# Hybrid decoder layer, fp32-accurate MLP: output tiles, token-tile turns, second-weight sums, norm rows and last chunks rearranged

## The chip, the cores and the metric

The kernel runs on one core of a Trainium2 chip. The metric is the device time of one execution in microseconds (us), as a median of several runs; lower is better. The core has five engines that run their own instruction queues: TensorE (PE, matrix products; its weight loads are listed as PEld), VectorE (DVE), ScalarE (ACT), GpSimd (POOL) and SyncE (SP, which here only issues DMAs). ACT and POOL issue DMAs too, each on its own queue. On chip there are the SBUF (128 partitions) and the PSUM, whose banks of 128x512 fp32 take the matrix products.

## The reference, cut to what matters

One layer for 1024 tokens of width 1024. A mixer (sliding-window attention beside a gated delta net) comes first; the change begins at its output projection and reaches to the end:

```python
mixed = (sigmoid(g_a) * y_a + sigmoid(g_b) * y_b) @ w_out[l]
x = _layer_norm(ALPHA * x + (1.0 + gt1) * mixed, ln1_g[l], ln1_b[l])
u2 = x * (1.0 + sc2) + sh2
h = jnp.square(jax.nn.relu(u2 @ w_ff1[l] + b_ff1[l]))          # 1024 -> 4096
x = _layer_norm(ALPHA * x + (1.0 + gt2) * (h @ w_ff2[l] + b_ff2[l]), ln2_g[l], ln2_b[l])
```

Everything is fp32 in and out.

## The kernel before

**Products.** An fp32 product is made of three faster ones: each operand is split into a high part (a rounded copy, made by ACT) and a low part (the remainder, made by DVE); PE adds high x high, high x low and low x high into one bank. The helper split_s (L213 and on) does it: ACT copies at once (L215), and DVE subtracts "lag" matmuls later (L216). Names such as wh and wl (weights), mh, ml, u11h and u11l (tokens) are such parts, and sp in the second layer.

**Seven products instead of eight.** Both MLP layers split their matrices in two by two blocks and use seven block products, whose operands are sums and differences of blocks. So DVE also forms sums of token tiles (T1 to T4), of the first weights (f_sums, f_sums2), of the hidden activations (h_sums, h_sums2, stored to the DRAM array hf_d), and of the second weights (t_make, stored to the DRAM array wt_d). The sums and differences are add_ (L1516) and sub (L1407).

**The order by hand.** Everything that DVE and ACT do beside the products is put into their queues by an events list: at(p, f) runs f when the count of matmuls has reached p, and after(n, f) runs it n matmuls later. So the order on PE, DVE and ACT is what the numbers say; an engine that waits holds up all that stands behind it in its queue. The order on the DMA queues of SP and POOL is settled by the framework when the kernel is built. E0 is the count at the start of the output projection of the mixer, F0 = E0 + 384 that at the start of the first MLP layer, and G0 = F0 + 1344 that of the second.

**Projection (E0 to F0).** Four segments of 96 matmuls give the eight token tiles of 128 tokens. mix_done (L1356 and on) adds the residual and takes the sums for the norm; ACT takes the root, DVE norms the tile, and then the tile is transposed ("turned") by PE (u2_turn, L1379) four 128x128 blocks at a time into a bank "b"; ACT puts each turned block from there into SBUF (L1382, "rawu<-b"), with the scale and the shift of the MLP. quad_split and t_split split the result, and the sums T1 to T4 are formed between (t_one, t_sums). Tiles 0 to 3 are turned in pairs of a first-half and a second-half tile, in blocks of 128x256 on ACT; tiles 4, 5, 6 and 7 one by one, in blocks of 128x128.

**First layer (F0 to G0).** 16 pairs of weight tiles ("pairs" 0 to 15), seven products each, 12 matmuls of 128x512 a product (L1841). The first five pairs (EARLY) run in an order of their own in which the products that need only early token tiles stand first. Each product ends in a bank with the name mm, a, b or c. ACT copies it with the bias into a "t" tile (part, L1558), or DVE adds it to one (full, L1516); ACT squares it (L1566, L1567; a last block L1577, L1578) and stores it to hf_d (L1554). The pool has six "t" tiles of 128x512, used in turn; one comes free when its store has landed and its other readers are done. t_load brings the second weights of pair n into two "wx" tiles and half an "sb" tile (on POOL's queue), t_make forms three differences "wx<-wx" and one "sb<-sb,wx" from them and stores them on the same queue.

**Second layer (G0 to the end).** 56 chunks of 24 matmuls (L1901). Each chunk loads an activation tile from hf_d and a weight tile ("sraw"): chunks 0 and 1 through ACT's queue, the others through SP's; s_split splits both. rows_load brings six rows of 128x1024 (gates and norm parameters, broadcast to all partitions); rows_sums combines three of them. The last seventh of the chunks goes chunk by chunk over four token tiles up to the last LAST = 4 chunks, which go tile by tile, so that a tile's gate, residual, norm and store (gated, norm2) can run while PE is on the next one. The last tile is cut in two halves of 256.

## Time and profile before

| | |
|---|---|
| median of 3 runs (lowest to highest) | 1829.93 us (1829.84 to 1831.34) |
| the profiled execution | 1830.36 us, span 1828.5 us, mean granted clock 0.994 |
| up to the first MLP layer | 0 to 1195.86 us |
| first layer, pairs 0 to 4 and the start of pair 5 | 1195.86 to 1300.75 us |
| first layer, the rest | 1300.75 to 1510.59 us |
| second layer | 1510.59 to 1818.49 us |
| after the last matmul | 1818.49 to 1828.5 us |

The span runs from the first to the last instruction of the profiled execution; 1.86 us lie around it. PE is busy nearly all the time, so the profile is read for the short moments in which PE waits. Rows of the timeline give start, duration, engine, line, operation, "out<-in" by the program's names, the shapes, and in brackets the idle time ahead of it with what ended it. Rows of the waits give the total, the number and the longest. Rows of the windows give, for a stretch, its length and each engine's busy time and instructions (PE, PEld, DVE, ACT, POOL), the granted clock, the DMA engines' share and the rate in GB/s.

### The profile page before, as it was taken

What the parts mean: (1) busy time and instruction counts of PE and PEld (TensorE: products, weight loads), DVE (VectorE), ACT (ScalarE), POOL (GpSimd) and SP (SyncE); (2) the same over time, 40 slices, a digit from 0 to 9 for tenths busy, and PEclk for the clock granted to TensorE, in tenths of its full rate; (3) what the DMA queues carried; (4) which work ended last, traced back from release to release, by engine and by line L of the source; (5) the groups of instructions that cost most, each with busy time, mean ns of one, the idle gap of its engine ahead of it and who ended that gap; (6) DMA issues with size and microseconds to landing.
All of it is one profiled execution on the core that took longest, in us unless ns stands there. A gap on an engine that the chain in (4) does not pass through costs nothing.

```text
span 1828.5 us, 26178 instructions
## 1 busy us (share of the span) xinstructions
PE 1806.0 (99%) x9161; PEld 1513.3 (83%) x9161; DVE 1262.5 (69%) x2377; ACT 1023.9 (56%) x2325; POOL 307.9 (17%) x464
## 2 busy tenths in 40 slices
PE   8999999999999999999999999999999999999997
PEld 6988888888888888888888888877888887888886
DVE  6688688888854666666644445887777766676697
ACT  4699678888864555555544222485555554434341
POOL 0233234453340000000001100012221120000000
PEclk8999999999999999999999999999999999999999
DMA  9756723232266555554447434369887779655571
GB/s 277 205 199 207 225 67 98 63 111 70 73 218 152 157 158 152 146 165 141 147 146 252 155 127 161 115 202 332 290 277 263 258 271 390 242 185 185 206 254 47
DMA packets 262670, 337.74 MB, mean 185 GB/s; under 512 B 26261, under 2 KB 171366, under 8 KB 262282
## 3 DMA queue, kind: packets, MB, share of 16 engines
q1 hardware_dynamic: 223210, 212.94, 37.1%
q0 software_dynamic: 31184, 106.34, 17.4%
q10 hardware_dynamic: 8144, 16.78, 2.6%
q8 instruction: 72, 1.18, 0.3%
q14 instruction: 60, 0.49, 0.1%
HBM read 231.40 MB, written 102.51 MB: 183 GB/s over the span
## 4 chain that ended last, share of the span: by engine, by line
PE 88%; DVE 3%; ACT 3%; DMA 2%; issue 0%; POOL 0%; ACTq 0%; DVEq 0%; POOLq 0%
PE mm L248 40%; PE mm L1841 7%; PE mm L1901 6%; PE b L1841 4%; PE b L1901 4%; PE a L1901 4%; PE a L1841 2%; PE mm L1470 2%; PE c L1901 2%; PE c L880 2%; PE a L1470 1%; DMA hf_d<-t 1%; PE mm L186 1%; PE mm L187 1%; PE mm L188 1%; PE a L806 1%
## 5 line engine op out<-in xcount | busy, mean ns | idle before, releaser
L248 PE MATMUL mm<-uh,wl 128*128 128x512 f32 x800 | 330.1, 413 | 0.0
L248 PE MATMUL mm<-ul,wh 128*128 128x512 f32 x800 | 314.7, 393 | 0.0
L248 PE MATMUL mm<-uh,wh 128*128 128x512 f32 x800 | 313.9, 392 | 0.0
L216 DVE TENSOR_TENSOR sp<-sraw,sp 128x1024 fp32r<-128x1024 f32 x112 | 132.8, 1220 | 77.9 <-ACT sp L215 77.8
L215 ACT ACTIVATE sp<-sraw 128x1024 fp32r<-128x1024 f32 x112 | 112.7, 1054 | 123.5 <-PE b L1901 75.3
L248 PEld LDWEIGHTS mm<-ul,wh 128*128 128x128 f32 x800 | 150.2, 188 | 31.8
L248 PEld LDWEIGHTS mm<-uh,wl 128*128 128x128 f32 x800 | 150.8, 188 | 26.3 <-issue 1.0
L248 PEld LDWEIGHTS mm<-uh,wh 128*128 128x128 f32 x800 | 150.9, 189 | 25.3 <-issue 1.0
L1901 PE MATMUL mm<-sp 128*128 128x512 f32 x528 | 137.0, 390 | 1.4 <-DVE sp L216 1.3
L1901 PEld LDWEIGHTS mm<-sp 128*128 128x128 f32 x528 | 98.5, 188 | 22.6 <-DVE sp L216 2.0
L216 DVE TENSOR_TENSOR wl<-wr,wh 128x1024 fp32r<-128x1024 f32 x81 | 99.4, 1228 | 8.5 <-ACT wh L215 8.4
L215 ACT ACTIVATE wh<-wr 128x1024 fp32r<-128x1024 f32 x81 | 85.2, 1052 | 22.1 <-PE c L1470 13.8
L1901 PE MATMUL a<-sp 128*128 128x512 f32 x336 | 92.6, 389 | 0.0
L813 DVE CUSTOM_DVE_ANT_0 nscore<-a,amask,nsink 128x256 f32<-128x256 f32 (+1 forms) x128 | 54.5, 464 | 44.8 <-PE a L806 44.5
L1901 PE MATMUL b<-sp 128*128 128x512 f32 (+1 forms) x336 | 80.0, 374 | 0.0
L1901 PEld LDWEIGHTS a<-sp 128*128 128x128 f32 x336 | 63.1, 188 | 13.1
L1142 ACT ACTIVATE vn<-a,brk 128x128 f32<-128x128 f32 x64 | 23.5, 368 | 89.0 <-PE a L1140 89.0
L1901 PEld LDWEIGHTS b<-sp 128*128 128x128 f32 x336 | 60.5, 188 | 11.2
L216 DVE TENSOR_TENSOR wl<-fraw,wh 128x1024 fp32r<-128x1024 f32 x43 | 52.6, 1223 | 23.2 <-ACT wh L215 22.9
L824 POOL TENSOR_TENSOR sm<-sm 128x256 f32<-128x256 f32 x56 | 50.8, 906 | 105.2 <-ACT sm L820 76.9
L215 ACT ACTIVATE wh<-fraw 128x1024 fp32r<-128x1024 f32 x43 | 45.0, 1056 | 33.1 <-PE b L1841 16.3
L820 ACT ACTIVATE sm<-nscore,stat 128x257 f32<-128x257 f32 (+1 forms) x128 | 62.0, 488 | 2.7 <-DVE stat L813 2.5
(522 smaller groups left out, 4662.0 us busy)
## 6 DMA issues: line engine op xcount, KB each, us to landing
wr<-in_w_in_dram SPq DMA_DIRECT2D x60, 512.0 KB, 3.8
sraw<-hf_d SPq DMA_DIRECT2D x54, 512.0 KB, 4.5
adaw<-in_w_ada_dram SPq DMA_DIRECT2D x73, 256.0 KB, 4.7
fraw<-in_w_ff_dram SPq DMA_DIRECT2D x32, 512.0 KB, 5.2
sraw<-wt_d SPq DMA_DIRECT2D x32, 512.0 KB, 4.3
hf_d<-t ACTq DMA_DIRECT2D x48, 256.0 KB, 3.5
wt_d<-wx POOLq DMA_DIRECT2D x48, 256.0 KB, 3.0
sraw<-in_w_ff_dram SPq DMA_DIRECT2D x22, 512.0 KB, 5.6
```

Of the source, the lines that this page charges most:

```text
L186: T.matmul(t, lhsT=wh[:, k, :], rhs=xh[k][:, sl], start=k == 0, stop=False)
L215: A.activation(out=hi, in_=src, func=AF.Copy)
L216: after(lag, lambda: V.tensor_tensor(out=lo, in0=src, in1=hi.bitcast(F32), op=ALU.subtract))
L248: T.matmul(ts[half], lhsT=w[:, k, :], rhs=xx[k][:, sl], start=k == 0 and m == 0, stop=k == KT - 1 and m == 2)
L813: V.tensor_tensor_reduce(out=ns[:, i, 1:1 + W], in0=sc[:, i * 2 * P:i * 2 * P + W], in1=amask[:, mo:mo + W], scale=-1.0, scalar=nsink[:, 2 ...
L820: A.activation(out=sm[:, i, 0:1 + W], in_=ns[:, i, 0:1 + W], func=AF.Exp, scale=-1.0, bias=st[:, i:i + 1], accum_out=st[:, 2 + i:3 + i])
L824: G.tensor_tensor(out=sm[:, :, 1 + P:1 + 2 * P], in0=sm[:, :, 1:1 + P], in1=sm[:, :, 1 + P:1 + 2 * P], op=ALU.add)
L880: T.matmul(av[:, 0:256], lhsT=vt[:, b, :], rhs=p_[:, m, :], start=p_ is full and m == 0, stop=p_ is prods[-1][1] and m == 1)
L1142: after(1, lambda: A.activation(out=vn, in_=Wp[:, 0:P], func=AF.Copy, scale=brk[:, n, h:h + 1]))
L1470: T.matmul(pt, lhsT=m[k][:, tok], rhs=w[:, k % 2, :], start=k == 0 and w is wh and m is mh, stop=k == KT - 1 and m is ml)
L1841: T.matmul(pt, lhsT=a[:, k0 + k, :], rhs=b[k], start=begin and k == 0 and x_ == 0, stop=k == 3 and x_ == 2, skip_group_check=True)
L1901: T.matmul(to, lhsT=a[:, f, t * P:(t + 1) * P], rhs=b[:, f, lo:up], start=(begin or own) and s % NS == 0 and f == 0 and x_ == 0, stop=s % ...
```

## The change

It has eight parts, in the words of the program:

1. Eight "t" tiles instead of six. To make room, the small tiles tri, trim, amask and the eleven tiles made by small() move from a pool that lives to the end into gp (through brief), a pool that is closed soon after the projection begins.
2. Tiles 4 and 5, and tiles 6 and 7, are turned together: pair_turn makes four turns of two blocks of each tile, and each turn is put by two ACT copies of 128x256 (16 copies of 128x128 a pair before). pair_quad and pair_split split pieces of the pair, in the order T1, block 22, sums, T2, T3, T4. The times of the events (29 and 44 after the last tile's end, the lags of mix_done and of the root) follow.
3. The first tile of the first weights is split 37 matmuls sooner, into four "t" tiles (W0).
4. t_make of the 16 pairs stands at the places of a table (MAKE), t_load 40 matmuls ahead of each.
5. The six norm rows go through SP's queue, one every 24 matmuls from G0 + 62; rows_sums moves from G0 + 60 to G0 + 190.
6. LAST = 5: five last chunks tile by tile.
7. The last chunk's two splits stand 6 matmuls apart instead of 10.
8. The norms of the first three tiles of the last product run over the whole width in one piece.

```diff
@@ -51,6 +51,11 @@
     big = ctx.enter_context(tc.tile_pool(name="big", bufs=1))
     ps = ctx.enter_context(tc.tile_pool(name="ps", bufs=2, space=PSUM))
     dram = ctx.enter_context(tc.tile_pool(name="dram", bufs=1, space=DRAM))
+    gp_pool = tc.tile_pool(name="gp", bufs=2, side="right")
+    gpool = gp_pool.__enter__()
+
+    def brief(shape, name):
+        return gpool.tile(shape, F32, name=name, bufs=1)
 
     def psum(tag, bufs, name=None):
...
-    tri = const.tile([P, P], F32, name="tri")
+    tri = brief([P, P], "tri")
...
@@ -1309,8 +1312,8 @@
     for f in range(KT):
         stream_unit(oh, ol, yb_done(f))
 
-    def row(dst, src):
-        nc.gpsimd.dma_start(out=dst, in_=src[None, :].partition_broadcast(P))
+    def row(dst, src, q=None):
+        (q or nc.gpsimd).dma_start(out=dst, in_=src[None, :].partition_broadcast(P))
 
     E0 = count[0]
...
         rq = r[:, halves[q]]
-        tm = pe.tile([P, HALF], F32, tag="t", name="tm", bufs=6)
+        tm = pe.tile([P, HALF], F32, tag="t", name="tm", bufs=8)
...
         V.bn_aggr(out=st[:, 0:2], in_=parts[:, t].rearrange("p q s -> p (q s)"))
-        lag = {6: 26, 7: 12}.get(t, 1)
+        lag = {6: 26, 7: 8}.get(t, 1)
...
@@ -1419,26 +1422,70 @@
             for k in range(4):
                 at(p + 12 + 3 * (4 * kh + k), t_split, j, kh, k)
 
+    rawp = {}
+
+    def pair_turn(u, ks):
+        if ks[0] == 0:
+            for kh in range(2):
+                rawp[kh, u] = big2.tile([P, 4, 2, P], F32, tag=f"{'hl'[kh]}{6 + u}", name="rawp")
+        tp = psum("b", 2)
+        for i, k in enumerate(ks):
+            for v in range(2):
+                T.transpose(tp[:, (2 * i + v) * P:(2 * i + v + 1) * P], rs[TILE[u][2 + v]][:, k * P:(k + 1) * P], ident)
+
+        def put(i, k):
+            A.activation(out=rawp[k // 4, u][:, k % 4].rearrange("p j c -> p (j c)"),
+                         in_=tp[:, 2 * i * P:2 * (i + 1) * P],
+                         func=AF.Identity, scale=sc2[:, k:k + 1], bias=sh2[:, k:k + 1])
+        for i, k in enumerate(ks):
+            after(2 + i, put, i, k)
+
+    def pair_quad(name, kh, u):
+        for i in range(2):
+            src = rawp[kh, u][:, 2 * i:2 * i + 2].rearrange("p k j c -> p k (j c)")
+            hi, lo = (t[i][:, :, 2 * P:4 * P] for t in U[name, "t"])
+            split_s(hi, lo, src, 4)
+
+    def pair_one():
+        sub(V, rawp[0, 1], rawp[0, 1], rawp[0, 0])
+
+    def pair_sums():
+        sub(V, rawp[1, 1], rawp[1, 1], rawp[0, 1])
+        sub(V, rawp[0, 0], rawp[1, 1], rawp[0, 0])
+        sub(V, rawp[1, 0], rawp[1, 0], rawp[1, 1])
+
+    def pair_split(kh, u, k):
+        hi, lo = (t[4 * kh + k].rearrange("p (j u c) -> p j u c", j=4, u=2)[:, 2:4, u, :] for t in (mh, ml))
+        split_s(hi, lo, rawp[kh, u][:, k], 3)
+
+    def pair_done(u, p):
+        for kp in range(4):
+            at(p + (4, 8)[u] * kp, pair_turn, u, (2 * kp, 2 * kp + 1))
+        if u == 0:
+            at(p + 8, pair_quad, "11", 0, 0)
+            at(p + 17, pair_quad, "21", 1, 0)
+            return
+        at(p + 14, pair_one)
+        for k in range(4):
+            at(p + 20 + 3 * k, pair_split, 0, 1, k)
+        at(p + 32, pair_quad, "22", 1, 1)
+        at(p + 39, pair_sums)
+        for n, (kh, v) in enumerate(((1, 1), (0, 0), (1, 0))):
+            for k in range(4):
+                at(p + (42, 66, 80)[n] + 3 * k, pair_split, kh, v, k)
+
     def u2_done(t, p):
 
         u = t in TILE[1]
         j = TILE[u].index(t)
-        if j < 2:
-            if not u:
-                return
+        if j == 3:
+            pair_done(u, p)
+        elif j < 2 and u:
             for kp in range(4):
                 at(p + 5 * kp, u2_turn, j, (0, 1), (2 * kp, 2 * kp + 1))
             at(p + 13, quad_split, j, "11", 0, 0)
             at(p + 23, quad_split, j, "21", 1, 0)
             u2_rest(j, p + 24)
-            return
-        for kp in range(2):
-            at(p + 6 * kp, u2_turn, j, (u,), range(4 * kp, 4 * kp + 4))
-        if u:
-            u2_rest(j, p + 14)
-        else:
-            at(p + 8, quad_split, j, "11", 0, 0)
-            at(p + 14, quad_split, j, "21", 1, 0)
 
     at(E0 + 15, open_pe)
...
@@ -1456,9 +1503,17 @@
         split_s(hl[0], hl[1], r[0])
 
 
+    W0 = []
+
+    def w_first():
+        raw = raws.pop(0)[0]
+        for kh in range(2):
+            W0.append([pe.tile([P, 4, P], F32R, tag="t", name="w0", bufs=8) for _ in "hl"])
+            split_s(W0[kh][0], W0[kh][1], raw[:, 4 * kh:4 * kh + 4, :], 5)
+
     w_more()
-    for p in [1, 13] + [SEG * s + o for s in (0, 2) for o in (61, 73, 86, 98)] + [3 * SEG + o for o in (79, 100, 118, 134, 154)]:
-        at(E0 + p, w_go)
+    for p in [1, 13] + [SEG * s + o for s in (0, 2) for o in (61, 73, 86, 98)] + [3 * SEG + o for o in (42, 98, 118, 134, 154)]:
+        at(E0 + p, w_first if p == 3 * SEG + 42 else w_go)
         at(E0 + p + 8, w_more)
 
...
@@ -1490,10 +1545,10 @@
                 for pt, t in zip(pts, ts):
                     mix_mm(pt, slice(t * P, (t + 1) * P), c)
             for pt, t in zip(pts, ts):
-                lag = 14 if s == 2 and t > 5 else 10 if s == 3 and t == 7 else 1
+                lag = {(2, 6): 14, (2, 7): 56, (3, 7): 10}.get((s, t), 1)
                 at(max(count[0] + lag, E0 + 28), mix_done, s % 2 == 1, q, t, pt)
                 if s % 2 == 1:
-                    at(count[0] + 1, u2_done, t, count[0] + {4: 30, 5: 36, 6: 48, 7: 42}.get(t, 34) - lag + 1)
+                    at(count[0] + 1, u2_done, t, count[0] + {5: 29, 7: 44}.get(t, 34) - lag + 1)
 
 
...
@@ -1673,10 +1728,10 @@
         for j, t in enumerate((t1, t2, t3, t4)):
             nc.gpsimd.dma_start(out=wt_d[j, n], in_=t)
 
+    MAKE = (172, 246, 320, 394, 484, 552, 620, 693, 767, 842, 916, 990, 1068, 1139, 1214, 1288)
     for n in range(NPAIR):
-        p = pos[n, 1] - 8 if n > EARLY else F0 + 100 + 68 * n
-        at(p, t_load, n)
-        at(p + 36, t_make, n)
+        at(F0 + MAKE[n] - 40, t_load, n)
+        at(F0 + MAKE[n], t_make, n)
 
 
...
@@ -1724,11 +1779,12 @@
             acc[t] = p2f.tile([P, D], F32, name=f"acc{t}", bufs=1)
         stats["all"] = p2f.tile([P, NT, 22], F32, name="stats", bufs=1)
 
-    def rows_load():
-        for n, (name, src) in enumerate((("gt2", gt_d[1]), ("G2", ln1_g), ("B2", b_ff2), ("lb", ln1_b), ("g2", ln2_g),
-                                         ("b2", ln2_b))):
-            rows_[name] = wp.tile([P, D], F32, tag="wl" if n % 2 else "wh", name=name)
-            row(rows_[name], src)
+    ROWS = (("gt2", gt_d[1]), ("G2", ln1_g), ("B2", b_ff2), ("lb", ln1_b), ("g2", ln2_g), ("b2", ln2_b))
+
+    def rows_load(n):
+        name, src = ROWS[n]
+        rows_[name] = wp.tile([P, D], F32, tag="wl" if n % 2 else "wh", name=name)
+        row(rows_[name], src, nc.sync)
 
     def rows_sums():
...
@@ -1796,7 +1852,7 @@
         after(3, rest)
 
     p15 = pos[NPAIR - 1, 1]
-    LAST = 4
+    LAST = 5
     for s in range(7 * NS):
         p = G0 + 24 * s
         at((p15 + 16, p15 + 28, p15 + 62, p15 + 64)[s] if s < 4 else p - 96 - 28, s_load, s)
@@ -1804,13 +1860,14 @@
             if s < 2:
                 q = p15 + (52, 68)[s] + 8 * j
             elif s >= 6 * NS:
-                q = p - (94 if s > 6 * NS else 70) + 10 * j
+                q = p - (94 if s > 6 * NS else 70) + (6 if s == 7 * NS - 1 else 10) * j
             else:
                 q = p - 46 + 10 * j
             at(q, s_split, s, j)
     at(G0 + 2, open_p2f)
-    at(G0 + 3, rows_load)
-    at(G0 + 60, rows_sums)
+    for n in range(6):
+        at(G0 + 62 + 24 * n, rows_load, n)
+    at(G0 + 190, rows_sums)
     for t in range(NT):
         at(G0 + 200 + 60 * t, rr_load, t)
...
@@ -1836,9 +1893,10 @@
         for k in range(4):
             for x_ in range(3):
                 run_events(count[0])
-                (wh, wl), (uh_, ul_) = WF[i, w], U[mv]
+                (wh, wl), (uh_, ul_) = W0[k0 // 4] if (i, w) == (0, "a") else WF[i, w], U[mv]
+                kk = k if (i, w) == (0, "a") else k0 + k
                 a, b = ((wh, uh_), (wh, ul_), (wl, uh_))[x_]
-                T.matmul(pt, lhsT=a[:, k0 + k, :], rhs=b[k], start=begin and k == 0 and x_ == 0,
+                T.matmul(pt, lhsT=a[:, kk, :], rhs=b[k], start=begin and k == 0 and x_ == 0,
                          stop=k == 3 and x_ == 2, skip_group_check=True)
                 count[0] += 1
...
@@ -1931,7 +1989,7 @@
                         for f in range(2):
                             step(s, f, t, lo, up)
                     after(1, gated, 4 + t, lo, up, 1 + i, (tail[0] if i else bank[t])[:, lo:up])
-                after(1, norm2, 4 + t, [(HALF, D), (0, HALF)], 1 + len(cuts) - 1)
+                after(1, norm2, 4 + t, [(0, D)] if t < 3 else [(HALF, D), (0, HALF)], 1 + len(cuts) - 1)
             break
         for _ in steps(range(s0 + 1, s0 + NS - 1), False):
             pass
```

How three places move in the engines' queues. On ACT, in the first layer, ahead of the split of the second weight tile of pair 0 (rows "wh<-fraw"; "mh<-..." are splits of token sums, "t<-..." output tiles). Before:

```order
L215 ACTIVATE mh<-rawu 128x256 x9
L1558 ACTIVATE t<-b,cols 128x512
L1566 ACTIVATE t<-t 128x512
L1567 ACTIVATE t<-t 128x512
L1554 DMA hf_d<-t 128x512
L215 ACTIVATE wh<-fraw 128x1024 x2
```

And now:

```order
L1622 ACTIVATE t<-t 128x512
L1609 DMA hf_d<-t 128x512
L220 ACTIVATE wh<-fraw 128x1024 x2
L220 ACTIVATE mh<-rawp 128x2x128 x3
L1613 ACTIVATE t<-b,cols 128x512
L220 ACTIVATE mh<-rawp 128x2x128
L1621 ACTIVATE t<-t 128x512
L1622 ACTIVATE t<-t 128x512
L1609 DMA hf_d<-t 128x512
L220 ACTIVATE mh<-rawp 128x2x128 x4
```

Nine token splits stood ahead of the two weight splits; now eight of the token splits stand behind them.

On DVE, at pair 12 ("wl<-fraw" low parts of first weights, "x<-fraw" and "fraw<-fraw" their sums, "t<-t,mm" the addition that reads bank mm, "wx<-wx" and "sb<-sb,wx" the second weight sums). Before:

```order
L1516 TENSOR_TENSOR t<-t,a 128x512
L1407 TENSOR_TENSOR wx<-wx 128x512 x3
L1407 TENSOR_TENSOR sb<-sb,wx 128x512
L1407 TENSOR_TENSOR x<-fraw 128x512
L1516 TENSOR_TENSOR fraw<-fraw 128x512
L1407 TENSOR_TENSOR fraw<-fraw 128x512 x2
L216 TENSOR_TENSOR wl<-fraw,wh 128x1024
L1516 TENSOR_TENSOR t<-t,mm 128x512
```

And now:

```order
L1571 TENSOR_TENSOR t<-t,a 128x512
L1410 TENSOR_TENSOR x<-fraw 128x512
L1571 TENSOR_TENSOR fraw<-fraw 128x512
L1410 TENSOR_TENSOR fraw<-fraw 128x512 x2
L221 TENSOR_TENSOR wl<-fraw,wh 128x1024
L1410 TENSOR_TENSOR wx<-wx 128x512 x3
L1410 TENSOR_TENSOR sb<-sb,wx 128x512
L1571 TENSOR_TENSOR t<-t,mm 128x512
L221 TENSOR_TENSOR wd<-x,wd 128x512
```

The second weight sums have moved from ahead of the first weights' sums to between the low part and the addition "t<-t,mm".

On SP, at the start of the second layer ("sraw" are the chunks' loads, "hf_d<-..." stores of hidden activations, gt, G, B and lb norm rows). Now:

```order
L1609 DMA hf_d<-t 128x512
L1648 DMA hf_d<-sa 128x2x512
L1609 DMA hf_d<-sb 128x512
L1761 DMA sraw<-hf_d 128x2x512
L1316 DMA gt_14752<-gt_d 128x1024
L1316 DMA G_14790<-in_ln_g_dram 128x1024
L1609 DMA hf_d<-t 128x512
L1648 DMA hf_d<-sa 128x2x512
L1609 DMA hf_d<-sb 128x512
L1316 DMA B_14828<-in_b_ff_dram 128x1024
L1316 DMA lb<-in_ln_b_dram 128x1024
L1767 DMA sraw<-in_w_ff_dram 128x2x512
```

Before, the same place had no norm rows; they stood at the end of POOL's queue, the last four there around the last stores of second weight sums:

```order
L1313 DMA gt_14683<-gt_d 128x1024
L1313 DMA G_14685<-in_ln_g_dram 128x1024
L1313 DMA B_14687<-in_b_ff_dram 128x1024
L1313 DMA lb<-in_ln_b_dram 128x1024
L1674 DMA wt_d<-wx 128x512 x3
L1674 DMA wt_d<-sb 128x512
L1313 DMA g_14691<-in_ln_g_dram 128x1024
L1313 DMA b_14693<-in_ln_b_dram 128x1024
```

The rows gt, G, B and lb now stand ahead of the weight load of chunk 2 on SP's queue, and g and b stand there further on, behind five more chunks.

More of the change, by code (lines that the diff above doesn't have):

```diff
@@ L270, in hybrid_layer_kernel @@
     ul = [big.tile([P, S], F32R, tag=f"l{k}", name=f"ul{k}") for k in range(KT)]
-    gp_pool = tc.tile_pool(name="gp", bufs=2, side="right")
-    gpool = gp_pool.__enter__()
     kp_pool = tc.tile_pool(name="kp", bufs=1, side="right")
@@ L489, in small @@
     def small(name):
-        return const.tile([P, NT, 8], F32, name=name)
+        return brief([P, NT, 8], name)
     beta, g, negegc, ekd, last = (small(n) for n in ("beta", "g", "negegc", "ekd", "last"))
@@ L1545, in tile_of @@
     def tile_of(i, c):
-        t = tls[i, c] = pe.tile([P, HALF], F32, tag="t", name="t", bufs=6)
+        t = tls[i, c] = pe.tile([P, HALF], F32, tag="t", name="t", bufs=8)
         return t
@@ L1828, in hybrid_layer_kernel @@
         w, k0, mv, ab, begin = PROD[m]
-        if m == 1 and i < EARLY:
+        if m == 1 and 0 < i < EARLY:
             run_events(count[0])
```

4 lines of the change are left out of this document (2 added, 2 removed).

## The prediction

> **What bounds the kernel now.** I read the busy shares first, then the waits of TensorE (PE), then the windows by stage, and last the timeline around each wait.
>
> ```profile
> PE 1806.0 (99%) x9161; PEld 1513.3 (83%) x9161; DVE 1262.5 (69%) x2377; ACT 1023.9 (56%) x2325; POOL 307.9 (17%) x464
> PE b L1841 <- ACT t L1558: 2.0, 1, 2.0
> 1000.00:1100.00 100.00, 100.00 (x442) 82.79 (x442) 47.18 (x64) 30.63 (x40) 9.03 (x17) 1.00 0.45 144
> 1195.86:1300.75 104.89, 100.97 (x438) 80.80 (x436) 86.52 (x135) 65.68 (x117) 19.84 (x37) 0.98 0.80 267
> ```
>
> PE is busy for 99% of the 1828.5 us, so no other engine's total matters: only moments when PE stands still can be won, and the change removes no matmul worth counting. The largest wait within the last third is a single one of 2.0 us (total, times, longest). In a quiet stage (first window) PE starts 442 matmuls in 100 us, one per 0.227 us. The second window begins where the first-layer MLP starts; there DVE is 82% busy, DMA at 0.80 of its engines, and the granted clock falls to 0.98. The waits that the change can reach lie there, just ahead of it, at the start of the second layer and at the end.
>
> **What one wait costs.** The timeline gives start, duration, and in brackets the idle time and its releaser.
>
> ```profile
> 1276.87 0.39 PE L1841 MATMUL c<-u22h,wl 128*128 128x512 f32 x1
> 1279.24 0.50 PE L1841 MATMUL b<-mh,wd 128*128 128x512 f32 x1 [1.99 <-ACT t L1558]
> 1279.58 0.39 PE L1841 MATMUL b<-ml,wd 128*128 128x512 f32 x1
> ...
> 1280.53 1.05 PE L1841 MATMUL b<-mh,wd 128*128 128x512 f32 x2
> 1281.39 0.63 PE L1841 MATMUL b<-ml,wd 128*128 128x512 f32 x1
> ...
> 1283.92 0.40 PE L1841 MATMUL a<-ml,wh 128*128 128x512 f32 x1
> ```
>
> From 1276.87 to 1279.58 two starts take 2.71 us instead of 0.454: the wait costs 2.26, or the bracket's 1.99 plus 0.27 for filling the pipeline again. I price every bracket below as idle + 0.27. Behind this one matmuls start 0.43 apart (two from 1280.53 to 1281.39): from 1280.53 to 1283.92 eight take 3.39 us instead of 1.82, another 1.57. That is half rate right behind a wait, so I count it with the wait: 3.83 us.
> The Trainium skill (page "TensorE: Matmul & The Clock Gate", section "HAM oscillation") drops the clock only for idle gaps over about 3.4 us. Here 1.99 us of idle was followed by half rate, so the row and the page differ; by the page the 1.57 would not go with the wait, and the sum would be 1.57 smaller.
>
> **Eight output tiles instead of six.**
>
> ```profile
> 1249.31 0.50 PE L1841 MATMUL mm<-mh,wd 128*128 128x512 f32 x1 [0.40 <-ACT t L1558]
> 1263.36 0.50 PE L1841 MATMUL mm<-mh,wd 128*128 128x512 f32 x1 [0.15 <-ACT t L1558]
> ACT t L1558 <- DMA hf_d<-t: 12.4, 3, 5.3
> 1278.51 0.69 ACT L1558 ACTIVATE t<-b,cols 128x512 f32<-128x512 f32 x1 [5.29 <-DMA hf_d<-t]
> ```
>
> ACT's bias copy (L1558) empties the bank that PE needs next. It needs a "t" tile, and the oldest is held by a store to hf_d still under way: 12.4 us of ACT waiting in three cases, the last until 1278.51, 0.73 us before PE's 1279.24. With two more tiles the slot wanted is one that was released two allocations sooner, so I take all three as gone: 3.83 + (0.40 + 0.27) + (0.15 + 0.27) = **4.9 us**. Bounds: 0 if a store is still later, 4.9 if none is. What is late next is PE itself. The room comes from tiles of earlier stages and costs no instruction.
>
> **Token tiles in pairs.**
>
> ```profile
> 1190.91 0.66 PE L1379 MATMUL b<-ident,r 128*128 128x128 f32 x4 [0.32 <-ACT rawu L1382]
> 1193.97 0.66 PE L1379 MATMUL b<-ident,r 128*128 128x128 f32 x4 [1.01 <-ACT rawu L1382]
> 1141.68 1.02 ACT L1382 ACTIVATE rawu<-b,sh,sc 128x256 f32<-128x256 f32 x2 [4.53 <-PE b L1379]
> 1191.35 2.92 ACT L1382 ACTIVATE rawu<-b,sh,sc 128x128 f32<-128x128 f32 x8
> ```
>
> A turn (four transposes) waits for the bank that ACT's puts still read; the puts are 128x128 at 0.37 each (eight in 2.92). Turned as a pair, a turn is emptied by two puts of 128x256, which tiles 0 to 3 use already: two in 1.02. So a turn is empty after 1.0 us instead of 1.5, a pair's eight puts take 4.1 us of ACT against 5.8 for the sixteen of before, and the turns stand further apart (4 and 8 matmuls from one to the next, with half as many blocks to empty). Gain (0.32 + 0.27) + (1.01 + 0.27) = **1.9 us**; bounds 0 and 1.9. Pair (6,7) starts its first turn 35 positions into the MLP, right behind the norm of tile 7, earlier relative to its data: 0 to 0.6 us (a short wait like 0.32 + 0.27), I take **-0.3**.
>
> **The first pair's second weight tile.**
>
> ```profile
> 1219.88 2.88 ACT L215 ACTIVATE mh<-rawu 128x256 fp32r<-128x256 f32 x9 [0.40 <-ACT t L1567]
> 1226.04 0.50 PE L1841 MATMUL c<-mh,wh 128*128 128x512 f32 x1 [0.17 <-ACT wh L215]
> 1227.30 0.50 PE L1841 MATMUL c<-mh,wl 128*128 128x512 f32 x1 [0.53 <-DVE wl L216]
> ```
>
> The product waits first for the high part of a weight tile (ACT), then for its low part (DVE). Nine token splits, 2.88 us, stand ahead of the high part on ACT; in the changed order eight token splits that stood ahead stand behind it. It was late by 0.17 and its low part by 0.53, both less than 2.88: (0.17 + 0.27) + (0.53 + 0.27) = **1.2 us**, bounds 0 and 1.2. Late next are the token splits now behind it, wanted by the products after this one.
>
> **Second weight sums at an even pace.** The same 16 sums, moved. In the first pairs DVE has 82% of work; a sum beside a deadline would cost up to its own length. I take **-0.5**, bounds 0 and -4 (rival 1). At pair 12 the table puts the sum between the weight's low part and the addition that frees bank "mm". The same place without the sum, two pairs later in the trace of before:
>
> ```profile
> 1480.18 2.01 DVE L1407 TENSOR_TENSOR wx<-wx 128x512 f32<-128x512 f32 x3
> 1483.58 0.69 ACT L1558 ACTIVATE t<-b,cols 128x512 f32<-128x512 f32 x1 [0.84 <-PE b L1841]
> 1486.83 1.23 DVE L216 TENSOR_TENSOR wl<-fraw,wh 128x1024 fp32r<-128x1024 f32 x1 [1.13 <-ACT wh L215]
> 1487.97 0.68 DVE L1516 TENSOR_TENSOR t<-t,mm 128x512 f32<-128x512 f32 x1
> 1488.82 0.39 PE L1841 MATMUL mm<-mh,wh 128*128 128x512 f32 x1
> ```
>
> The sum is four operations, 2.65 us (2.01 + about 0.65). Today it runs before the low part (1480.18). Without it there the low part can come earlier, but its high part follows ACT's 1483.58 copy: about 1484.2 + 1.05 = 1485.25 instead of 1486.83. Then 1485.25 + 1.14 + 2.65 = 1489.04 for the addition, against 1487.97: 1.07 later. PE now starts 0.17 after the addition's end (1487.97 + 0.68), so it waits 1.07 - 0.17 = 0.9 and 0.1 for refilling: **-1.0 us**; bounds -2.5 (no earlier low part) and 0 (a low part as much earlier as the sum is long).
>
> **Norm rows on SP's queue.**
>
> ```profile
> 1516.36 0.50 PE L1901 MATMUL mm<-sp 128*128 128x512 f32 x1 [0.16 <-ACT sp L215]
> 1517.62 1.45 PE L1901 MATMUL mm<-sp 128*128 128x512 f32 x5 [0.76 <-DVE sp L216]
> 1523.89 1.43 PE L1901 MATMUL mm<-sp 128*128 128x512 f32 x5 [0.49 <-DVE sp L216]
> q0 software_dynamic: 1077, 3.80, 42.0%
> q10 hardware_dynamic: 1510, 2.87, 30.0%
> sraw<-in_w_ff_dram ACTq DMA_DIRECT2D x2, 512.0 KB, 17.6
> ```
>
> Chunks 1 and 2 of the second layer wait for splits, which wait for loads. Between 1490 and 1516 POOL's queue (q0) took 42% of the DMA engines, ACT's (q10), which loads chunks 0 and 1, 30%; ACT's weight loads needed 17.6 us. Six rows of 512 KB, most of q0's load, now go one by one through SP's queue, the first two behind the first activation load and the last two five chunks later. With POOL's queue down to the weight sums' stores I estimate ACT's loads at 10 to 14 us instead of 17.6, some 4 us sooner where 1 is missing. Gain 0.43 + 1.03 + 0.76 = **2.2 us**; bounds -4 and 2.2. For what stays of chunk 2's wait I take **-0.4**.
> The Trainium skill (page "DMA: Bandwidth & Descriptors", section "Issuing engines are not separate DMA queues") says that DMAs of all issuing engines interleave on the same 16 engines. By that the move wins nothing and only the two rows put later do; it is part of rival 2.
>
> **Five last chunks tile by tile.**
>
> ```profile
> 1816.77 1.72 PE L1901 MATMUL b<-sp 128*128 128x256 f32 x13
> 1813.33 0.68 DVE L1778 TENSOR_TENSOR acc<-a,gt 128x512 f32<-128x512 f32 x1
> 1819.04 0.42 DVE L1778 TENSOR_TENSOR acc<-c,gt 128x256 f32<-128x256 f32 x1
> 1820.30 0.41 DVE L1778 TENSOR_TENSOR acc<-b,gt 128x256 f32<-128x256 f32 x1
> 1793.46 2.34 DVE L216 TENSOR_TENSOR sp<-sraw,sp 128x1024 fp32r<-128x1024 f32 x2
> ```
>
> PE ends at 1816.77 + 1.72 = 1818.49, but DVE is on the tile before until 1819.04 and takes up PE's last result at 1820.30, 1.81 late. A tile costs DVE 5.71 us (1813.33 to 1819.04) and PE 24 x 0.227 = 5.45; with five chunks PE takes 30 x 0.227 = 6.8, so DVE is waiting when PE ends, and takes the last result some 0.2 us behind it: **1.6 us**, bounds 0 and 1.8. The price: the last chunk is wanted sooner. The five chunks start at about 1818.49 - 120 x 0.227 = 1791.3, and the first tile reads the fifth after 24 matmuls, at 1796.7; its low part ends now at 1793.46 + 2.34 = 1795.80, and the split pitch of 6 instead of 10 keeps or advances that. The cover is 0.9 us; if it is gone the cost is what is lacking, up to 1 us.
>
> **The sum.** 4.9 + 1.9 + 1.2 + 2.2 + 1.6 = 11.8 won; 0.3 + 0.5 + 1.0 + 0.4 = 2.2 lost; net 9.6. The profiled execution took 1830.36 us (its span 1828.5 and 1.86 around it), so 1820.8; the median shown, 1829.93, is 0.43 below it, so **1820.3 us**.
>
> **Rivals.**
>
> 1. DVE becomes the bound in the first five pairs.
>
> ```profile
> 1261.58 1.42 DVE L1407 TENSOR_TENSOR wx<-wx 128x512 f32<-128x512 f32 x2 [0.37 <-DMA wx<-in_w_ff_dram]
> DMA to landing us min/median/max: 2.3/4.2/5.2
> DMA to landing us min/median/max: 2.3/4.5/7.4
> ```
>
> The sum at 1261.58 waited 0.37 for its load, with all of DVE queued behind it. For: 82% busy. Against: the pace of the first sums goes from one per 68 matmuls to one per 74, 15.4 to 16.8 us. Were each of five sums to cost 0.9 instead of 0.1, 4 us: **1824.3**. Chance 0.14.
> 2. The rows delay chunks 2 and 3 instead, which load through SP, or moving them wins nothing. The four rows ahead of them are 2.1 MB; by q10's row 2.87 MB were 30% of 26 us, 0.37 MB per us of the whole DMA, so they take 5.7 us, and I call about a third of it not hidden. The 2.2 go, and up to 2 more: **1822.5 to 1824.5**. For: 42, 30 and more per cent add up to a full DMA either way. Against: the rows can leave before the chunks' own tiles are free. Chance 0.18.
> 3. Tiles were not what ACT waited for, since the stores only slow each other: the 4.9 stay, **1825.2**. Against: the three waits name the store. Chance 0.06.
> 4. Slower. A sum's buffers turn over once per interval: stores of the last (first landing row, up to 5.2) and then the loads (second row, up to 7.4), 12.6 us, must fit between two sums, 16.8 - 2.65 = 14.15 us. If eight tiles, freed from waiting, crowd DMA (0.80 busy now) so that stores and loads together exceed 14.15 by 4, DVE stands 4 us in front of each of five pairs; PE has some 2 us of cover, waits 2 as at 1279.24 and then runs half rate: 5 x 3.83 = 19 us less the 9.6: 1829.93 + 9.6, or **1839.5**. It decides from about 16 us for the chain; measured is 12.6 at worst. Chance 0.04.
>
> **How the numbers follow.** Forecast 0.58 (its own range 1817 to 1823), rivals 0.14, 0.18, 0.06 and 0.04. The likeliest is 1820.3. With every unknown at its better bound (no loss at all) the time is 1818; further waits too small for my list could bring 2 more, so the range begins at 1816. It ends at 1826, past rivals 1 to 3, and leaves out the fourth and mixtures. A measurement can tell 0.2%, 3.7 us, from no change: faster is below 1826.3, slower above 1833.6. Rivals 1 to 3 alone are faster; two of them together are within 0.2%. Hence faster 0.89, same 0.06, slower 0.05.
>
> **What would show it.** Tiles: no ACT wait on hf_d<-t between 1196 and 1300, no matmuls 0.43 apart. Pairs: no PE wait on the puts. Rows: chunk 1 without a wait. End: DVE takes the last result within 0.3 us of PE's end. Against me: a PE wait on "t<-t,mm" in pair 12 over 0.9, DVE waiting for wx for 1 us or more per pair, or new waits at chunks 2 and 3.

## The result, and the profile after

The changed kernel takes 1820.36 us (median of four runs, 1819.38 to 1821.1) beside 1829.88 us before (four runs, 1828.75 to 1831.34): a ratio of 0.9947 with a 95% interval of 0.9930 to 0.9964. It is faster, and the forecast of 1820.3 us was right. The terms behind the sum were not all right, though, and the experiments show one of them wrong by several us.

First the waits of PE from 1100 us on, after the change (total, times, longest):

```profile
PE mm L1899 <- DVE t L1571: 0.8, 1, 0.8
PE b L1899 <- DVE t L1571: 0.5, 1, 0.5
PE b L1382 <- ACT rawu L1385: 0.2, 1, 0.2
PE c L1899 <- DVE wl L221: 0.2, 1, 0.2
PE c L1899 <- ACT t L1613: 0.2, 1, 0.2
```

The wait of 2.0 us for an output tile, those for the puts of the last token tiles and those at the first chunks of the second layer are gone; the one for the low part of the first pair's second weight tile (wl) is down from 0.53 to 0.22 us. The largest is now the forecast wait at pair 12, on the addition behind the second weight sum:

```profile
1441.63 2.01 DVE L1410 TENSOR_TENSOR wx<-wx 128x512 f32<-128x512 f32 x3
1443.68 0.69 DVE L1410 TENSOR_TENSOR sb<-sb,wx 128x512 f32<-128x512 f32 x1
1444.29 0.68 DVE L1571 TENSOR_TENSOR t<-t,mm 128x512 f32<-128x512 f32 x1
...
1445.03 0.50 PE L1899 MATMUL mm<-mh,wh 128*128 128x512 f32 x1 [0.80 <-DVE t L1571]
```

0.80 and 0.27 for refilling are 1.07 us; the forecast had 1.0. Next the DMA queues ahead of the second layer, 1485 to 1511 us (q1 is SP's, q10 ACT's, q0 POOL's):

```profile
q1 hardware_dynamic: 2293, 5.38, 58.2%
q10 hardware_dynamic: 1664, 3.15, 31.5%
q0 software_dynamic: 415, 1.35, 12.8%
sraw<-in_w_ff_dram ACTq DMA_DIRECT2D x2, 512.0 KB, 12.6
```

POOL's share fell from 42.0 to 12.8%, and ACT's weight load for chunk 1 (the one of the two whose landing the profile tells) lands in 12.6 us instead of 17.6 (10 to 14 were forecast). Chunk 1 no longer waits. Last the end of the kernel:

```profile
1808.77 1.84 PE L1959 MATMUL b<-sp 128*128 128x256 f32 x14
1808.79 0.42 DVE L1834 TENSOR_TENSOR acc<-c,gt 128x256 f32<-128x256 f32 x1
1810.65 0.42 DVE L1834 TENSOR_TENSOR acc<-b,gt 128x256 f32<-128x256 f32 x1 [0.52 <-PE b L1959]
```

PE ends at 1810.61, and DVE, idle for 0.52 us, takes the last result 0.04 us later (1.81 before).

To see where the time went I cut both profiles at the first matmul of the projection, at the first of each MLP layer, at PE's end and at the end of the span. This table also holds the experiments, since single executions begin differently and only the stretch from the projection on can be compared to a few tenths:

| profile | projection starts | projection | first layer | second layer | rest | from the projection on |
|---|---|---|---|---|---|---|
| before | 1100.69 | 95.17 | 314.73 | 307.90 | 9.98 | 727.78 |
| after | 1101.27 | 93.71 | 310.07 | 305.56 | 8.01 | 717.35 |
| after, again | 1100.54 | 93.69 | 310.02 | 305.53 | 8.01 | 717.24 |
| before + eight tiles | 1101.90 | 95.15 | 310.44 | 307.74 | 9.96 | 723.29 |
| before + eight tiles + even pace | 1101.92 | 95.17 | 309.73 | 307.60 | 9.99 | 722.48 |
| before + eight tiles + rows on SP | 1106.27 | 95.30 | 309.76 | 306.82 | 10.06 | 721.94 |
| after, tiles turned singly | 1104.04 | 95.36 | 311.74 | 305.53 | 8.00 | 720.63 |
| after, old pace of the sums | 1102.88 | 93.77 | 317.27 | 305.53 | 8.02 | 724.59 |
| after, rows on POOL | 1101.03 | 93.69 | 310.03 | 306.62 | 8.83 | 719.16 |
| after, LAST = 4 | 1101.80 | 93.64 | 310.07 | 305.62 | 8.84 | 718.19 |
| after, first weight tile late | 1100.95 | 93.57 | 310.91 | 305.53 | 8.07 | 718.08 |
| after, entry 12 moved | 1101.76 | 93.77 | 308.95 | 305.53 | 8.00 | 716.24 |
| after, entries 3 and 12 moved | 1102.01 | 93.63 | 307.90 | 305.53 | 8.00 | 715.06 |
| the same, again | 1102.78 | 93.92 | 307.89 | 305.71 | 8.00 | 715.52 |

The change won 10.43 us there: 1.46 in the projection, 4.66 in the first layer, 2.34 in the second and 1.97 behind PE's end. The profiled execution of after happened to reach the projection 0.58 us later than that of before. That leaves 9.85 of the span.

### The profile page after: what moved, and what is told of

The parts are those of the page before. It is cut to its first block, busy times and chain, and to the rows that moved or that the text cites. A ratio compares the mean times of both kernels' runs of the same rounds, so it can differ in the third digit from the quotient of the medians.

```text
span 1818.6 us, 26129 instructions
## 1 busy us (share of the span) xinstructions
PE 1801.8 (99%) x9161; PEld 1512.8 (83%) x9161; DVE 1260.7 (69%) x2362; ACT 1017.5 (56%) x2304; POOL 304.2 (17%) x458
## 4 chain that ended last, share of the span: by engine, by line
PE 90%; DVE 3%; ACT 2%; DMA 1%; issue 1%; POOL 0%; ACTq 0%; DVEq 0%; POOLq 0%; SPq 0%
PE mm L253 40%; PE mm L1899 8%; PE mm L1959 7%; PE a L1959 4%; PE b L1899 4%; PE b L1959 4%; PE a L1899 3%; PE c L1959 2%; PE c L883 2%; PE mm L1525 1%; PE mm L191 1%; PE mm L192 1%; PE mm L193 1%; PE a L809 1%; PE a L1525 1%; PE a L808 1%
```

## The experiments

**1. Eight tiles alone.** The room and bufs=8 in the kernel before, nothing else.

```diff
-        t = tls[i, c] = pe.tile([P, HALF], F32, tag="t", name="t", bufs=6)
+        t = tls[i, c] = pe.tile([P, HALF], F32, tag="t", name="t", bufs=8)
```

> The kernel before with eight t tiles instead of six, and nothing else of the change. Theory (the bias copies waited for a tile held by a store): ACT's waits on hf_d<-t between 1196 and 1300 us go from 12.4 us to under 1, PE's waits of 1249, 1263 and 1279 go and no matmuls run 0.43 apart behind 1279; 4 to 5 us less than before, about 1825.2. Rival (the stores themselves are slow because DMA is full, so a tile more only moves the wait): ACT still waits for hf_d<-t by several us, less than 1.5 us gained.

Median 1827.39 us (12 runs, 1824.52 to 1830.15), ratio 0.9984 [0.9975, 0.9993]. In the profile ACT no longer waits for hf_d at all in the first layer, the three waits of PE and the half rate are gone, and the stretch is 4.49 us shorter. The mechanism is as stated, but the runs gain only 2.4 in the median and spread over 5.6 us. Two things in this profile could make the spread. DVE waits for second weights (waits of DVE in the first layer), where it waited 0.4 before:

```profile
DVE wx L1410 <- DMA wx<-in_w_ff_dram: 1.0, 1, 1.0
```

And ACT stands 5.69 us in the issue of one load (ACTq is ACT issuing a DMA), so that PE waits 0.54 us for its next copy; the timeline:

```profile
1491.24 5.69 ACTq L1715 DMA_DIRECT2D sraw<-in_w_ff_dram  x1
1499.19 0.50 PE L1844 MATMUL mm<-mh,wd 128*128 128x512 f32 x1 [0.54 <-ACT t L1561]
```

The first of the two also stands in the second profile of the changed kernel (1.0 us, experiment 9), whose five runs lie within 2.8 us, so it need not bring a spread.

**2. LAST back at 4.**

```diff
-    LAST = 5
+    LAST = 4
```

> The changed kernel with LAST back at 4, norms in one piece and splits 6 apart kept. Theory (DVE needs 5.7 us a tile and PE 5.45 with four chunks): DVE takes up PE's last result 1.6 to 2.0 us after PE ends instead of 0.04, and the time from PE's end to the end of the span is 9.6 to 10.0 us instead of 8.0; 1822.0 to 1822.4. Rival (the one-piece norm made the gain, or the end is bound by the last stores): within 0.5 us of the changed kernel.

Median 1822.06 us, ratio 0.9953 [0.9939, 0.9967]. The rest behind PE's end is 8.84, only 0.83 more than in after. The timeline of PE and DVE there:

```profile
1808.82 2.32 PE L1959 MATMUL b<-sp 128*128 128x256 f32 x18
1812.02 0.41 DVE L1834 TENSOR_TENSOR acc<-b,gt 128x256 f32<-128x256 f32 x1
```

DVE takes the last result 0.88 us after PE's end (1811.14), where it was 1.81 before. So the norm in one piece, kept here, has won the other 0.93. DVE works on the last three tiles without a pause for PE here, as it did before, and one of them takes 5.34 us instead of 5.71:

```profile
1805.43 0.69 DVE L1834 TENSOR_TENSOR acc<-a,gt 128x512 f32<-128x512 f32 x1
1810.77 0.42 DVE L1834 TENSOR_TENSOR acc<-c,gt 128x256 f32<-128x256 f32 x1
```

Both theories were half right. The halves depend on the order in which the parts are added, though: with five chunks PE gives a tile 6.8 us, more than the 5.71 that DVE needs with the norm in two pieces, so by these rows I estimate that LAST = 5 alone would win nearly all of it. That was not run. The median is higher by 1.7, 0.9 more than the trace accounts for; such differences lie within what the starts of executions scatter.

**3. Norm rows on POOL's queue again.**

```diff
-        row(rows_[name], src, nc.sync)
+        row(rows_[name], src, nc.gpsimd)
```

> The changed kernel with the six norm rows issued on POOL's queue again, their places in the program as changed. Theory (POOL's queue takes its own share of the DMA engines beside ACT's): ACT's two weight loads of chunks 0 and 1 take 16 to 18 us again instead of 12.6, PE waits 1 to 2 us for chunk 1 and some for chunk 2, 1.5 to 2.5 us more than the changed kernel, about 1822.4. Rival (all queues share the same DMA engines, the bytes ahead count, not the queue): ACT's loads stay at 12 to 13 us, no wait at chunk 1, within 0.5 us.

Median 1822.24 us, ratio 0.9954 [0.9942, 0.9967]. The DMA view, 1485 to 1511 us, and PE's waits from 1100 us on:

```profile
q10 hardware_dynamic: 1526, 2.90, 29.7%
q0 software_dynamic: 1124, 3.95, 39.5%
sraw<-in_w_ff_dram ACTq DMA_DIRECT2D x2, 512.0 KB, 16.6
```

```profile
PE mm L1959 <- DVE sp L221: 0.5, 2, 0.3
```

ACT's load for chunk 1 takes 16.6 us again, and PE waits at chunks 1 and 2: 0.5 us and twice the refilling, 1.06 us of the second layer. The rest after PE's end is 0.82 longer too, all behind DVE's last operation; why was not tried. So the queue counts: with the same rows on another queue ACT's load takes 4.0 us longer. The Trainium skill (page "DMA: Bandwidth & Descriptors", section "Issuing engines are not separate DMA queues") has the issuing engine save nothing but issue time; on that the trace differs (12.6 against 16.6 us).

The two rows that the change puts later, g and b, are not the main reason. POOL issues them at 1505.10 and 1505.64 here, the load lands at 1508.32, and between 1505.10 and then POOL's queue moves 0.28 MB, which is 0.7 us at the 409 GB/s of that stretch. What is not separated is the order: B and lb leave POOL's queue at 1491.64 and 1492.15, some 2 to 3 us sooner than they leave SP's in after (1493.70 and 1495.18). And the waits that came back are 1.06 us of the 2.34 by which the second layer got shorter; which edit won the rest was not tried.

**4. Pair 12's sum 8 matmuls earlier.**

```diff
-    MAKE = (172, 246, 320, 394, 484, 552, 620, 693, 767, 842, 916, 990, 1068, 1139, 1214, 1288)
+    MAKE = (172, 246, 320, 394, 484, 552, 620, 693, 767, 842, 916, 990, 1060, 1139, 1214, 1288)
```

> The changed kernel with pair 12's second weight sum 8 matmuls earlier (1060 instead of 1068), ahead of the low part of the first weights' split instead of between it and the addition that frees bank mm. Theory (the sum's 2.65 us stand in front of the addition): PE's wait of 0.80 us for t<-t,mm in pair 12 goes, 1.0 us less than the changed kernel, about 1819.3. Rival (DVE's total work in that stretch is what is late): a wait of 0.5 us or more stays at pair 12, for the addition or for the low part, and the time is within 0.4 us.

The wait is gone, and the first layer is 1.12 us shorter (308.95). The median, 1820.33 us (six runs, ratio 0.9941 [0.9928, 0.9954]), doesn't differ from the changed kernel's by more than the scatter.

**5. Eight tiles and the even pace**, in the kernel before. The table of experiment 4 in place of the old rule.

```diff
-        p = pos[n, 1] - 8 if n > EARLY else F0 + 100 + 68 * n
-        at(p, t_load, n)
-        at(p + 36, t_make, n)
+        at(F0 + MAKE[n] - 40, t_load, n)
+        at(F0 + MAKE[n], t_make, n)
```

> The kernel before with eight t tiles and the even table of second weight sums (pair 12's at 1060, so that its wait stays out). In the run with eight tiles alone the second weights landed at 1262.56 us for a sum that could start at 1260.99, at 1278.24 for one at 1278.0, and its times ran from 1824.5 to 1830.2. Theory (with PE no longer waiting, 68 matmuls a sum are too short for the loads, so DVE waits for wx by an amount that differs from run to run, and PE behind it at times at half rate): DVE never waits for wx, and the runs lie within 2 us of each other, at 1823.5 to 1826. Rival (the spread comes from the start of the second layer, where ACT stood 5.7 us in one DMA issue): the runs spread over 4 us or more again, median about 1827.

Median 1826.4 us (1824.7 to 1829.03), ratio 0.9981 [0.9972, 0.9991]. DVE waits 1.1 us for wx once, and the runs spread over 4.3 us: the theory missed. The rival's numbers came, but not with its cause: no issue of ACT takes longer than 0.86 us in this profile. The first layer takes 309.73 instead of 310.44, about what PE's wait at 1499 above cost with its refilling, and that wait is not there. So with tiles turned singly these profiles show no other gain of the even pace.

**6. Eight tiles and the rows on SP's queue**, in the kernel before (the edit of the change's part 5).

```diff
-    at(G0 + 3, rows_load)
-    at(G0 + 60, rows_sums)
+    for n in range(6):
+        at(G0 + 62 + 24 * n, rows_load, n)
+    at(G0 + 190, rows_sums)
```

> The kernel before with eight t tiles and the norm rows on SP's queue, the old pace of the second weight sums. Theory (the pace makes the spread): waits at chunks 1 and 2 go (about 2 us less than with eight tiles alone, median 1825), but the runs still spread over 4 us or more, and DVE waits for wx by 0.5 us or more. Rival (ACT's 5.7 us in a DMA issue ahead of the second layer makes the spread): ACT's issues take under 1.5 us, the runs lie within 2 us of each other, at 1821.5 to 1824.

Median 1826.12 us (1824.38 to 1829.91), ratio 0.9982 [0.9973, 0.9991]. The second layer is 0.92 us shorter than with eight tiles alone, not 2: ACT still stood 3.70 us in one issue, and the chunks still wait by 0.6 us. The runs spread as wide as ever. That does not decide on the rival, since the long issue that it blames did not go; experiment 5, with a spread of 4.3 us and no such issue in its profile, speaks against it. The profiled execution, at 1829.91 the slowest, shows where its time went: the projection starts at 1106.27, over 4 us later than in experiment 1, in code that neither experiment touches. PE's timeline in the mixer:

```profile
222.31 0.30 PE L808 MATMUL a<-khh,qs 128*128 128x128 f32 x1 [1.62 <-issue]
...
222.89 0.63 PE L253 MATMUL mm<-ul,wh 128*128 128x512 f32 x1
223.32 0.63 PE L253 MATMUL mm<-uh,wl 128*128 128x512 f32 x1
223.75 0.63 PE L253 MATMUL mm<-uh,wh 128*128 128x512 f32 x1
```

PE waits 1.62 us for nothing that the profile shows, and then eight matmuls start 0.43 apart. Between 200 and 230 us this execution falls 2.4 us behind that of experiment 1. It loses another 1.7 at a wait for a load, further on in the mixer:

```profile
561.03 0.65 PE L1064 MATMUL b<-T,L 64*64 64x64 f32 x14 [1.37 <-DMA T<-t_d]
```

At least part of the spread is therefore made in the mixer, ahead of the change.

**7. Two entries of the table moved**: 12 as in experiment 4, and 3 behind the two additions that it stood ahead of in pair 4.

```diff
-    MAKE = (172, 246, 320, 394, 484, 552, 620, 693, 767, 842, 916, 990, 1068, 1139, 1214, 1288)
+    MAKE = (172, 246, 320, 411, 484, 552, 620, 693, 767, 842, 916, 990, 1060, 1139, 1214, 1288)
```

> The changed kernel with two entries of the table moved: pair 12's sum from 1068 to 1060 and pair 3's from 394 to 411, behind the additions that free banks a and b. Theory (each of the two waits left in the changed kernel, 0.80 at pair 12 and 0.53 in pair 4, is one sum standing in front of an addition): both waits go, 1.0 and 0.8 us with refilling, 1.8 us less than the changed kernel, about 1818.5. Rival (the sum pushed back makes what stands behind it late, wd's low part or the next weight's): a new wait of 0.5 us or more near 1294, and about 1819.3.

Both waits are gone and no other came: the first layer takes 307.90, 2.17 less than in after. The median is 1820.1 us (five runs), ratio 0.9950 [0.9938, 0.9962]: not told apart from the changed kernel.

**8. The last four tiles turned singly**, as before, in the changed kernel (with the lags of before).

```diff
-            pair_done(u, p)
...
+        for kp in range(2):
+            at(p + 6 * kp, u2_turn, j, (u,), range(4 * kp, 4 * kp + 4))
...
-                     at(count[0] + 1, u2_done, t, count[0] + {5: 29, 7: 44}.get(t, 34) - lag + 1)
+                     at(count[0] + 1, u2_done, t, count[0] + {4: 30, 5: 36, 6: 48, 7: 42}.get(t, 34) - lag + 1)
```

> The changed kernel with the last four token tiles turned one by one again (old turns, old puts of 128x128, old times and lags). Theory: PE's waits for the puts (0.32 and 1.01 at the end of the projection) and for the first pair's second weight tile (0.17 and 0.53) come back, 1.9 + 1.2 - 0.5 for the rest of that wait that the changed kernel still has: 2.6 us more, about 1823.0. Rival (these waits went because the first weight tile is split earlier, not because of the turns): at most 1 us more.

Median 1824.37 us (12 runs, 1823.2 to 1831.7), ratio 0.9978 [0.9968, 0.9988]; the stretch is 3.28 us longer. From its waits of PE:

```profile
PE b L1382 <- ACT rawu L1385: 1.3, 2, 1.0
PE a L1907 <- DVE u21l L221: 1.0, 1, 1.0
PE c L1907 <- DVE wl L221: 0.5, 1, 0.5
PE c L1907 <- ACT wh L220: 0.4, 1, 0.4
```

The waits for the puts and for the first pair's weight tile are back. It is the turning in pairs, with the times that go with it, that took them away. The wait for a token tile's low part (u21l) was not there before, so 3.28 us is more than the pairs won.

**9 and 10. The changed kernel again, and the two entries again**, unaltered.

> The changed kernel once more, unaltered, beside the kernel with entries 3 and 12 of the table moved. In the profiles so far, the stretch from the start of the output projection to the end took 717.35 us in the changed kernel and 715.06 with the two entries moved, but the medians differ by 0.26 only; the time up to the projection went from 1101.0 to 1106.3 us between executions, though nothing is changed there. Theory (the start of the kernel, outside the change, sets the spread): the stretch from the projection on is 717.4 within 0.5 again, whatever the start; the median is 1820 to 1821.

> The same kernel as with the two table entries moved, again. Theory: from the projection on 715.1 within 0.5 us; the time is 1.5 to 2.5 us less than the changed kernel in the same round, about 1818.5. Rival (something in the moved order is late in most executions, and the one profile was a lucky one): the stretch is 716.5 or more, the median within 0.5 us of the changed kernel.

From the projection on, the changed kernel repeats within 0.11 us (717.24), the other within 0.46 (715.52). The times do not follow: 1820.3 us (five runs, 1819.4 to 1822.2) and 1821.6 us (six runs, 1816.83 to 1826.12), ratios 0.9947 [0.9936, 0.9959] and 0.9953 [0.9938, 0.9967]. The lowest time of all, 1816.83, is the moved table's, but so is a scatter of 9 us. What its slower runs lose is not settled: the two profiles of it are of runs at 1818.86 and 1820.05. It can't be called faster.

**11. The old pace of the second weight sums**, in the changed kernel.

```diff
-        at(F0 + MAKE[n] - 40, t_load, n)
-        at(F0 + MAKE[n], t_make, n)
+        p = pos[n, 1] - 8 if n > EARLY else F0 + 100 + 68 * n
+        at(p, t_load, n)
+        at(p + 36, t_make, n)
```

> The changed kernel with the second weight sums at their old places (one per 68 matmuls in the first pairs, then one per pair). Theory of the prediction (the even pace wins nothing by itself and costs 1.0 at pair 12): the wait at pair 12 is not there, DVE waits about 1 us more for wx in the first pairs, which PE sees by 0.5 us or less: from the projection on 716.5 to 717.5, within 1 us of the changed kernel. Rival (with eight tiles and no waits of PE, 15.4 us a sum are too short for stores and loads of 12 to 14 us): DVE waits for wx by 2 us or more, PE waits behind it by 1 us or more, at times at half rate; 719 or more from the projection on.

Median 1826.62 us (11 runs, 1824.76 to 1829.22), ratio 0.9978 [0.9969, 0.9986], 6.3 us over the changed kernel. In the profile, taken of the slowest of these runs, the first layer takes 7.20 us more (317.27), although the wait at pair 12 is gone. The timeline of DVE and PE at the first sum of second weights, and behind it the windows (clock, DMA share and GB/s stand last):

```profile
1237.09 2.06 DVE L1410 TENSOR_TENSOR wx<-wx 128x512 f32<-128x512 f32 x3 [4.20 <-DMA wx<-in_w_ff_dram]
1242.34 0.50 PE L1900 MATMUL a<-mh,wh 128*128 128x512 f32 x1 [4.29 <-ACT wh L220]
1243.84 0.80 PE L1900 MATMUL a<-mh,wl 128*128 128x512 f32 x1 [0.76 <-DVE wl L221]
...
1244.86 0.63 PE L1900 MATMUL a<-ml,wh 128*128 128x512 f32 x1
...
1249.55 0.52 PE L1900 MATMUL mm<-mh,wh 128*128 128x512 f32 x1
```

```profile
1236.00:1244.00 8.00, 2.94 (x13) 1.81 (x11) 6.74 (x10) 2.12 (x2) 3.78 (x7) 0.94 0.60 211
1244.00:1250.00 6.00, 6.00 (x15) 4.72 (x16) 5.72 (x9) 3.24 (x6) 0.00 (x0) 0.51 0.98 281
```

DVE stands 4.20 us at the first sum; the sums of the first weights are queued behind it, ACT waits for those, PE for ACT, and then PE runs at a granted clock of 0.51 until 1249.9. Why the load is late is seen on POOL, in the kernel before, in this one and in the changed kernel:

```profile
1218.82 0.54 POOL L1662 DMA_DIRECT2D wx<-in_w_ff_dram  x1 [14.28 <-DVE ml L216]
1222.99 0.55 POOL L1663 DMA_DIRECT2D wx<-in_w_ff_dram  x1 [3.64 <-DVE ml L216]
```

```profile
1230.10 0.53 POOL L1717 DMA_DIRECT2D wx<-in_w_ff_dram  x1 [4.38 <-DVE ml L221]
1232.58 0.54 POOL L1718 DMA_DIRECT2D wx<-in_w_ff_dram  x1 [1.95 <-DVE ml L221]
```

```profile
1228.44 0.53 POOL L1717 DMA_DIRECT2D wx<-in_w_ff_dram  x1 [4.38 <-DVE ml L221]
1230.92 0.54 POOL L1718 DMA_DIRECT2D wx<-in_w_ff_dram  x1 [1.95 <-DVE ml L221]
```

The wx tiles use the space of turned token tiles (both carry the tags h6 and l6 in the kernel), and wait for the last splits of these ("ml"). Turned in pairs, the token tiles hold the space until T3 and T4 are split, and the first loads leave 9.6 to 11.3 us later than before (0.8 of it because the layer starts later in this execution). In the changed kernel they leave at the same places in the layer. The old place of the first sum, 136 matmuls into the layer, is then too early; the table has it at 172, 8.2 us later.

**12. The first weight tile split late**, at its old places and in a weight buffer.

```diff
-    for p in [1, 13] + [SEG * s + o for s in (0, 2) for o in (61, 73, 86, 98)] + [3 * SEG + o for o in (42, 98, 118, 134, 154)]:
-        at(E0 + p, w_first if p == 3 * SEG + 42 else w_go)
+    for p in [1, 13] + [SEG * s + o for s in (0, 2) for o in (61, 73, 86, 98)] + [3 * SEG + o for o in (79, 100, 118, 134, 154)]:
+        at(E0 + p, w_go)
```

> The changed kernel with the first tile of the first weights split at its old place again (79 and 100 instead of 42 and 98, in a weight buffer instead of four t tiles). The prediction gave this part no gain of its own. Theory (it only takes work out of the stretch in which the last token tiles are turned): PE waits at the start of the first layer by 0.2 to 0.5 us as before (0.28 and 0.20 there), up to 0.7 us more from the projection on. Rival (the split stands in front of the pairs' puts or in front of the norm of tile 7): 1 to 3 us more, with waits for the first turns of a pair.

Median 1820.95 us, ratio 0.9951 [0.9939, 0.9963]; the stretch is 0.73 us longer, with a wait of 0.36 us for the first tile's low part at 1200.95 and 0.3 more at the first pair's second weight tile. The theory held, and by the trace this part has a gain of its own; the median, 0.6 higher, can't tell it from the scatter.

## Why the prediction was right, and which step failed

- **Eight tiles, 4.9 us.** Held: 4.49 in the trace (the medians gain 2.4), and the half rate went with the wait. The rule "no PE-idle gaps >~3.4µs" (the Trainium skill, page "TensorE: Matmul & The Clock Gate", section "HAM oscillation") would let a gap of 1.99 us pass; the trace disagrees here too.
- **Tiles in pairs, 1.9, and the first pair's second weight tile, 1.2, less 0.3.** Held as a mechanism, and a little high in size: the projection got 1.46 shorter, not 1.9, and at the weight tile a wait of 0.22 and its refilling stay, so some 0.75 of the 1.2 was won. Undone, the pairs cost 3.28, with a wait that was not there before. No wait was found at the first turn of tiles 6 and 7; the first turn of 4 and 5 takes 0.96 us instead of 0.60.
- **Even pace, -0.5 for the first pairs.** This is the step that failed. The prediction took the table as "the same 16 sums, moved", whose price is what they push aside, and compared only the distance from sum to sum. It never asked what holds the space of the wx tiles ahead of the first sum. The table is the cover that the pairs need: without it the changed kernel loses 7.20 us in the profile and 6.3 in the median, and the whole change would win some 3. Rival 4 had the right chain (loads late, DVE in front of the pairs, PE at half rate) but for the changed kernel, by DMA load, and in every early pair; it happens once, and by the space, and the change avoids it. The sum was not hurt, since the gain of the tiles and that of the pairs were counted as if their cover were given.
- **Pair 12, -1.0.** Held: 1.07, and 1.12 when the entry is moved.
- **Rows, 2.2 less 0.4.** Held in size: 2.34 for the second layer. The queue is shown for part of it: undone, it costs 1.06 at the chunks (and 0.82 behind PE's end). What won the rest of the 2.34 is open. That only the two rows put later would count (rival 2) did not come true.
- **Five last chunks, 1.6.** Held: 1.97 with all edits at the end. The prediction gave nothing to the norm in one piece, which wins about 0.9 by itself; on top of it LAST = 5 wins 0.83. LAST = 5 alone was not run.
- **Early split of the first weight tile**: nothing forecast, 0.73 found, in one trace.

So the total came out by terms that were mostly right, some of them too high (0.4 in the projection, 0.5 at the weight tile), a small one that was missed (0.7), and losses that did not come true (0.3 for tiles 6 and 7, 0.5 for the sums, 0.4 at chunk 2). That it agrees to a tenth of a us is luck: the starts of the profiled executions differ by more.

## What to carry to other kernels

When an edit keeps a buffer longer, follow its space to the next tile that is put there, and ask when that tile's load is now issued and who is queued behind its first use. A part that looks like a cost may be the cover of another part; test such parts by taking each out of the changed kernel, not only by adding each to the old one (the even pace added: under 1 us; taken out: 7). Where executions scatter by more than an edit is worth, cut the trace at the place where the edit begins and compare from there.
